# One-core two-layer decoder: layer 0's row maxima and their causal mask in one VectorE instruction with a wide mask

## The chip, the cores and the metric

The kernel runs on one core of one Trainium2 chip. A core has TensorE (PE, with the queue of its weight loads shown as PEld), VectorE (DVE), ScalarE (ACT), GpSimd (POOL) and SyncE (SP), each with its own queue of instructions. Matrix products are written to PSUM; the other operands lie in SBUF. The metric is the device time of one execution in microseconds (us).

## The reference

The program is a decoder trunk of two layers over 1024 positions of width 1024, all in fp32. Layer 0 mixes by multi-head latent attention with 12 heads (query and key 96 wide: 64 without position, 32 with rotary position; values 64 wide), layer 1 by sliding-window attention with sinks and a linear distance bias. Both run memory cross-attention beside it, an output projection and a squared-ReLU MLP. The change lies in layer 0's causal attention:

```python
def one_block(args):
    q_blk, n = args                                   # 128 queries of every head
    t_idx = n * Q_BLOCK + jnp.arange(Q_BLOCK)
    sc = jnp.einsum('bqhd,bkhd->bhqk', q_blk, k) * scale
    mask = k_idx[None, :] <= t_idx[:, None]
    sc = jnp.where(mask[None, None], sc, NEG)         # NEG = -1e30
    p = jax.nn.softmax(sc, axis=-1).astype(v.dtype)
    return jnp.einsum('bhqk,bkhd->bqhd', p, v)
```

The softmax subtracts the maximum of each query's row over the keys that it may see.

## The kernel before, in words

An fp32 matrix is split into a high and a low part (names ending in h and l; ACT makes the high part at L99, DVE the low part at L100), and a product of two such matrices is three products on PE. Layer 0's attention works on scores that are transposed, keys on the partitions and queries along the row, so that the exponentials can go straight into the product with the values. [...] So the maxima are made beforehand from a second, cheaper set of scores that is not transposed.

One "row" of a head is a block of 128 queries: `row_max(h, i)` is row i of head h. It multiplies the high parts of block i's queries with the keys up to and including that block's (`psx`, n = (i+1) x 128 columns, in products of at most 512 columns, L907). A bf16 product of an identity `identb` with a matrix `dmask`, which is 0 on and below the diagonal and -1e30 above it, adds the causal mask to the last 128 columns in PSUM (L908). DVE takes the maximum over the n columns and writes its negative to column i of the head's tile `m8` (`m` in the profile, L909). When a head's eight rows are there, `max_row(h)` transposes m8 on PE (`psxt`, L889), splits it, and two DMAs put it into partition 96 of the head's query tiles `qh`, `ql`. The keys have a row of ones there, so that each transposed score comes out with its maximum taken off.

The main loop goes over (head, block of 128 keys, half of the queries), 12 steps a head. A step has three score products (`pss`, L1030); on diagonal blocks DVE adds the transposed mask `dmaskT` in PSUM (L1038); ACT takes the exponential `p` (L1040); some blocks are split again into `ph`, `pl` (L99, L100). Some steps later the value products go into `pso` (L1060). The values' last 64 columns are ones, so that the row sums come out beside them. The table `WHEN` (L1144) says at which step which row of the next heads' maxima is made: from head 3 on in the order 7, 6, ... 0, psxt last, one row in about one step of the twelve. Rows 4 to 7 of those heads use one PSUM tile with one buffer, rows 0 to 3 share six smaller buffers with the scores. Head 0 has no loop to lie in: its eight rows stand among the last query projections (`psqn`, L109 to L111, copied out at L939) and use a PSUM tile with two buffers.

The outputs of heads are divided by their sums in groups (heads 0 to 5, 6 to 9, 10, 11). DVE takes the reciprocals `rc` (L1119), POOL's queue writes them to DRAM and reads them back spread over 64 partitions each (`rb`, two DMAs for a pair of heads and a half, L1112), and DVE multiplies with them (L1129). `rb` has four buffers.

Within an engine, the order of the instructions is set by a scheduler from the program's order, the dependences and its costs. So taking instructions away can also move others.

Of the kernel before, what the change touches and what calls it, by code (L numbers as in the profile page):

```python
# [9 lines left out]
F32 = mybir.dt.float32  # L10
F32R = mybir.dt.float32r
BF16 = mybir.dt.bfloat16
I32 = mybir.dt.int32
AF = mybir.ActivationFunctionType
ALU = mybir.AluOpType
AX = mybir.AxisListType.X
# [3 lines left out]
P = 128  # L20
D = 1024
S = 1024
# [5 lines left out]
NEG = -1e30  # L28
# [27 lines left out]
def trunk(  # L56
# [7 lines left out]
    nc = tc.nc  # L64
    x = x[0]
    out = out[0]
    mem = mem[0]

    def pool(name, side="left", space=None, bufs=1):
        kw = {"reuse_waits": "tile"}  # L70
        if space is not None:
            kw["space"] = space
        return tc.alloc_tile_pool(name=name, bufs=bufs, side=side, **kw)

    const = pool("const")
# [3 lines left out]
    def ps2(name):  # L79
        return psum[0].tile([P, 1024], F32, tag="s", bufs=2, name=name)  # L80

    def ps1(name):
        return psum[0].tile([P, 512], F32, tag="m", bufs=4 if len(psum) == 1 else 6, name=name)

    def psx(name):
        return ps2(name) if len(psum) == 1 else psum[0].tile([P, 1024], F32, tag="x", bufs=1, name=name)
# [9 lines left out]
    def split(src, hi, lo, scale=None):  # L96

        if scale is None:
            a = nc.scalar.activation(hi, src, AF.Copy)  # L99
            d = nc.vector.tensor_tensor(lo, src, f32(hi), ALU.subtract)  # L100
        else:
            a = nc.scalar.activation(hi, src, AF.Copy, scale=scale)
            d = nc.vector.scalar_tensor_tensor(lo, src, scale, f32(hi), ALU.mult, ALU.subtract)
        return a.ins, d.ins
# [19 lines left out]
    ident = const.tile([P, P], F32, name="ident")  # L124
    nc.gpsimd.memset(ident, 1.0)
    nc.gpsimd.affine_select(out=ident, in_=ident, compare_op=ALU.is_equal, fill=0.0, base=0, pattern=[[-1, P]], channel_multiplier=1)
    identb, dmask = [const.tile([P, P], BF16, name=n) for n in ("identb", "dmask")]
    dmaskT = const.tile([P, P], F32, name="dmaskT")

    def masks(pl):  # L130

        nc.vector.tensor_copy(identb, ident)
        for dst, sgn in ((dmask, 1), (dmaskT, -1)):
            m = pl.tile([P, P], F32, tag="mask", bufs=2, name=f"mask{sgn}")
            nc.gpsimd.memset(m, 0.0)
            nc.gpsimd.affine_select(out=m, in_=m, compare_op=ALU.is_ge, fill=NEG, base=0, pattern=[[-sgn, P]], channel_multiplier=sgn)
            nc.vector.tensor_copy(dst, m)

    eps_t = const.tile([P, 1], F32, name="eps_t")
    nc.gpsimd.memset(eps_t, EPS)  # L140
# [428 lines left out]
    pm = pool("pm", "right")  # L569
# [109 lines left out]
    with tc.issue_after(k_done):  # L679
        put_rope()  # L680
    mp[1].keys(kvt)
    masks(pm)

    for h in range(H):
        nc.gpsimd.memset(padl[(h % 2) * 64 : (h % 2) * 64 + 64, 1 + h // 2 : 2 + h // 2], 0.125 / SLOPES[h])
# [172 lines left out]
    def head_bufs(pl, i):  # L858
        bufs_.append([pl.tile([97, S], F32R, name=f"{n}{i}") for n in ("qh", "ql", "kh", "kl")])

    def head_ones(i):
        if i == 0:
            nc.gpsimd.memset(f32(bufs_[0][2][96:97]), 1.0)
            nc.gpsimd.memset(f32(bufs_[0][3][96:97]), 0.0)
        else:
            for e in (2, 3):
                nc.sync.dma_start(out=f32(bufs_[i][e][96:97]), in_=f32(bufs_[0][e][96:97]))


    def head_tiles(h):  # L870
        r = slice((h % 2) * 64, (h % 2) * 64 + 64)
        q32 = hb.tile([96, S], F32, tag="q32", bufs=1, name=f"q32_{h}")
        k32 = hb.tile([96, S], F32, tag="k32", bufs=1, name=f"k32_{h}")
        nc.sync.dma_start(out=q32[0:64], in_=qn[h // 2][r, :])
        nc.sync.dma_start(out=q32[64:96], in_=qr[h // 4][(h % 4) * 32 : (h % 4) * 32 + 32, :])
        nc.sync.dma_start(out=k32[0:64], in_=kn[h // 2][r, :])
        nc.sync.dma_start(out=k32[64:96], in_=krs)
        qh, ql, kh, kl = bufs_[h % 3]
        if h in (1, 2):
            head_ones(h)  # L880
        split(q32, qh[0:96], ql[0:96])
        split(k32, kh[0:96], kl[0:96])

    m8s = {}

    def max_row(h):
        qh, ql, kh, kl = bufs_[h % 3]
# [11 lines left out]
    def row_max(h, i):  # L899
        if h not in m8s:  # L900
            m8s[h] = hb.tile([P, NT], F32, tag="m8", bufs=2, name=f"m8_{h}")
        qh, ql, kh, kl = bufs_[h % 3]
        n = (i + 1) * P
        ps = psx(f"psx{h}_{i}") if i > 3 or len(psum) == 1 else ps1(f"psx{h}_{i}")
        for a in range(0, n, 512):
            b = min(a + 512, n)
            nc.tensor.matmul(ps[:, a:b], qh[0:96, i * P : (i + 1) * P], kh[0:96, a:b], start=True, stop=b < n, skip_group_check=True)  # L907
        nc.tensor.matmul(ps[:, n - P : n], identb, dmask, start=False, stop=True, skip_group_check=True)  # L908
        nc.vector.reduce_max(m8s[h][:, i : i + 1], ps[:, :n], axis=AX, negate=True)  # L909

    f0 = quad_tile("f0", "qn0")
    qn = [(f0, f1)[j // 4][:, j % 4, :] for j in range(6)]
# [8 lines left out]
    for j in range(6):  # L921
# [4 lines left out]
        ps = ps2(f"pskn{j}")  # L926
# [45 lines left out]
    for n in range(2, 12):  # L972
        q_nope(n // 2, n % 2)
        for i in range(2 * n - 4, min(2 * n - 2, NT)):
            row_max(0, i)
        if n == 7:
            max_row(0)
# [8 lines left out]
    for i in (1, 2):  # L986
        head_bufs(hb1, i)
    at = pool("at", "right")
    vbufs = []
    for i in range(2):  # L990
        vb = (at.tile([P, 4, 128], F32R, name=f"vh{i}"), at.tile([P, 4, 64], F32R, name=f"vl{i}"))
# [5 lines left out]
    def v_tiles(h):  # L997

        vh, vl = vbufs[h % 2]
        src = v[:, 0:4, h * 64 : (h + 1) * 64]  # L1000
        if h < 2:
            nc.gpsimd.memset(f32(vh[:, :, 64:128]), 1.0)
        nc.scalar.activation(vh[:, :, 0:64], src, AF.Copy)
        nc.vector.tensor_tensor(vl, src, f32(vh[:, :, 0:64]), ALU.subtract)
# [102 lines left out]

    def rc_pair(c, j, i):

        rb = at.tile([P, 512], F32, tag="rb", bufs=4, name=f"rb{c}_{j}_{i}")  # L1110
        for e in range(min(2, GRP[c + 1] - GRP[c] - 2 * j)):
            (nc.sync if c == 2 else nc.gpsimd).dma_start(out=rb[e * 64 : e * 64 + 64, :], in_=rc_d[c][2 * j + e, halves[i]].partition_broadcast(64))  # L1112
        return rb
# [18 lines left out]
    def v_full(h):  # L1132
        nc.vector.tensor_copy(vfs[h % 2][:, :, 0:64], v[:, :, h * 64 : (h + 1) * 64])

    wq = WoHalf(0, 0, quad_slots())
    v_tiles(0)
    v_full(0)
    head_tiles(1)

    LV, LB = 3, 5  # L1140
# [13 lines left out]
    for n in range(len(seq) + LB):  # L1154
# [3 lines left out]
        for lag, late in ((LB, True), (LV, False)):  # L1158
            if 0 <= n - lag < len(seq):
                a, b = values(*seq[n - lag], late)  # L1160
# [11 lines left out]
        for g, i in ahead.get(n, ()):  # L1172
            if i < NT:
                row_max(g, i)
            else:
                max_row(g)
        h, j = divmod(n, NB)
# [789 lines left out]
    def feat_mm(w, i, nm, between=None):  # L1967
        ps = ps1(f"psf{nm}_{i}")
        terms = [(w[0][:, k, :], w[1][:, k, :], *xn0.at(k, halves[i])) for k in range(KT)]
        if between is None:  # L1970
            mm3(ps, terms)
        else:
            mm3(ps, terms[:4], last=False)
            between()
            mm3(ps, terms[4:], first=False)
        return ps
# [194 lines left out]
    for n, (c0, sink, j) in enumerate(jobs):  # L2171
# [17 lines left out]
        for i in range(2):  # L2189
            ps = feat_mm(w, i, str(n + 2), None if n < 6 else lambda: next(swa))  # L2190
# [76 lines left out]
```

## Time and profile before

| quantity | value |
|---|---|
| time, median of 3 runs | 2105.88 us (2105.57 to 2107.6) |
| profiled execution, its own time | 2106.59 us |
| its span | 2104.7 us |
| granted TensorE clock, mean | 0.999 |
| matrix products and weight loads | 9842 each |

The span runs from the first to the last instruction of the profiled execution; its own time holds what lies around it too. Layer 0's attention loop starts at about 234 us and ends at about 460 us; head 0's rows stand at 217 to 226 us. A row of a timeline has start, length, engine, line, operation, output and inputs, shapes, and in brackets the idle time before it and who ended it. "x2" means that two such instructions of one kind follow each other. Products on PE overlap, so from one start to the next is less than a product's length.

### The profile page before, as it was taken

Reading aid. Unit: us, or ns where it says so; the run is one execution under the profiler, and the core shown is the slowest. Engines: PE = TensorE matmul, PEld = TensorE weight load, DVE = VectorE, ACT = ScalarE, POOL = GpSimd, SP = SyncE. Lnnn points to the kernel's source line nnn. Section 1 sums busy time; section 2 is a strip of 40 time slices with the busy share of each in tenths; the row PEclk is TensorE's granted clock in tenths of the full one; section 3 lists DMA queues with packets and bytes.
Section 4 is the critical chain, followed back from the end, with each engine's and each line's share of the span. In section 5 each row is a group of like instructions: output and inputs, shape, how many; then the busy total and the mean of one; then the engine's idle time right before and its main releaser. Section 6 shows DMA issues by size and latency. Waiting matters only on the chain.

```text
span 2104.7 us, 28997 instructions
## 1 busy us (share of the span) xinstructions
PE 2084.4 (99%) x9842; PEld 1690.5 (80%) x9842; DVE 1473.9 (70%) x2906; ACT 1112.7 (53%) x2405; POOL 147.4 (7%) x263
## 2 busy tenths in 40 slices
PE   9999999999999999999999999999999999999998
PEld 7888766678888888888888878778788888888887
DVE  8766677775977777976557634666977776976565
ACT  6654466656755444444445434776755444444453
POOL 1001001010000000000001133431000000000000
PEclk9999999999999999999999999999999999999999
DMA  6302223342355446945433634542355446944442
GB/s 218 98 1 76 61 67 92 92 136 100 103 178 165 149 138 231 327 152 156 138 117 104 156 91 123 140 139 81 108 172 165 152 140 235 327 148 155 118 118 90
DMA packets 181796, 292.35 MB, mean 139 GB/s; under 512 B 17691, under 2 KB 71824, under 8 KB 181648
## 3 DMA queue, kind: packets, MB, share of 16 engines
q1 hardware_dynamic: 175152, 272.07, 41.4%
q0 software_dynamic: 5168, 15.80, 2.2%
q10 hardware_dynamic: 1328, 2.63, 0.3%
q8 instruction: 77, 1.26, 0.3%
q14 instruction: 71, 0.58, 0.1%
HBM read 187.34 MB, written 81.18 MB: 128 GB/s over the span
## 4 chain that ended last, share of the span: by engine, by line
PE 90%; DVE 5%; ACT 2%; DMA 1%; issue 1%; POOL 0%; SPq 0%; DVEq 0%; ACTq 0%; POOLq 0%
PE psy L1843 6%; PE psy L1844 6%; PE psy L1842 6%; PE psu L1534 5%; PE psu L1536 5%; PE psu L1535 5%; PE psz L1843 4%; PE psz L1844 4%; PE psz L1842 4%; PE psv L1536 4%; PE psv L1534 4%; PE psv L1535 4%; PE pso L1060 4%; PE pss L1030 3%; PE pswo L111 3%; PE pswo L109 3%
## 5 line engine op out<-in xcount | busy, mean ns | idle before, releaser
L1040 ACT ACTIVATE p<-pss 128x512 f32<-128x512 f32 (+2 forms) x144 | 68.6, 486 | 69.6 <-DVE pss L1038 52.7
L99 ACT ACTIVATE g<-i 128x512 fp32r<-128x512 f32 x79 | 49.8, 631 | 102.8 <-PE psz L1843 45.7
L1842 PE MATMUL psy<-g 128*128 128x512 f32 x256 | 99.9, 390 | 0.0
L1844 PE MATMUL psy<-g 128*128 128x512 f32 x256 | 99.7, 390 | 0.0
L1843 PE MATMUL psy<-g 128*128 128x512 f32 x256 | 99.6, 389 | 0.0
L100 DVE TENSOR_TENSOR g<-i,g 128x512 fp32r<-128x512 f32 x79 | 55.7, 705 | 50.7 <-ACT g L99 50.7
L99 ACT ACTIVATE i<-mr 128x512 fp32r<-128x512 f32 x78 | 47.8, 629 | 72.7 <-PE psu L1535 20.9
L1060 PE MATMUL pso<-p,vf 128*128 128x512 f32 (+2 forms) x192 | 85.4, 527 | 0.5 <-ACT p L1040 0.5
L909 DVE TENSOR_REDUCE m<-psx 128x1 f32<-128x1024 f32 (+7 forms) x96 | 71.9, 751 | 20.0 <-PE psx L908 19.6
L99 ACT ACTIVATE uh<-i 128x512 fp32r<-128x512 f32 x66 | 41.6, 631 | 82.0 <-PE psz L1843 38.3
L100 DVE TENSOR_TENSOR uh<-i,uh 128x512 fp32r<-128x512 f32 x66 | 45.5, 690 | 46.2 <-ACT uh L99 46.1
L1842 PE MATMUL psz<-g 128*128 128x512 f32 x192 | 74.7, 389 | 0.0
L1843 PE MATMUL psz<-g 128*128 128x512 f32 x192 | 74.7, 389 | 0.0
L1844 PE MATMUL psz<-g 128*128 128x512 f32 x192 | 74.7, 389 | 0.0
L1433 ACT ACTIVATE mr<-mr,gcol 128x256 f32<-128x256 f32 (+1 forms) x160 | 63.9, 476 | 13.9 <-DMA mr<-in_mlp_w_up_dram 13.9
L100 DVE TENSOR_TENSOR i<-mr,i 128x512 fp32r<-128x512 f32 x78 | 53.5, 686 | 23.7 <-ACT i L99 23.7
L1030 PE MATMUL pss<-qh,kh 97*128 97x512 f32 (+2 forms) x144 | 67.8, 473 | 0.0
L1030 PE MATMUL pss<-ql,kh 97*128 97x512 f32 (+2 forms) x144 | 58.2, 404 | 0.0
L1754 DVE TENSOR_TENSOR mqq<-mqf,mqq 128x512 f32<-128x512 f32 x64 | 43.0, 685 | 20.1 <-DMA mqf<-in_mlp_w_down_dram 20.0
L1842 PEld LDWEIGHTS psy<-g 128*128 128x128 f32 x256 | 48.1, 188 | 9.9
L1843 PEld LDWEIGHTS psy<-g 128*128 128x128 f32 x256 | 48.1, 188 | 9.9
L1844 PEld LDWEIGHTS psy<-g 128*128 128x128 f32 x256 | 48.1, 188 | 9.9
(648 smaller groups left out, 6858.3 us busy)
## 6 DMA issues: line engine op xcount, KB each, us to landing
i<-hd SPq DMA_DIRECT2D x154, 256.0 KB
hd<-uh SPq DMA_DIRECT2D x76, 256.0 KB
hd<-ul SPq DMA_DIRECT2D x76, 256.0 KB
mr<-in_mlp_w_up_dram SPq DMA_DIRECT2D x36, 512.0 KB
hd<-x SPq DMA_DIRECT2D x72, 256.0 KB
mr<-hd SPq DMA_DIRECT2D x70, 256.0 KB
d<-in_mlp_w_up_dram SPq DMA_DIRECT2D x32, 512.0 KB
mqf<-in_mlp_w_down_dram SPq DMA_DIRECT2D x32, 512.0 KB
```

Source lines behind the costliest of these rows:

```text
L99: a = nc.scalar.activation(hi, src, AF.Copy)
L100: d = nc.vector.tensor_tensor(lo, src, f32(hi), ALU.subtract)
L909: nc.vector.reduce_max(m8s[h][:, i : i + 1], ps[:, :n], axis=AX, negate=True)
L1030: return lambda: nc.tensor.matmul(o, a, b, skip_group_check=True, **kw)
L1040: nc.scalar.activation(p[:, c0:], ps, AF.Exp, scale=SC)
L1060: mms.append(lambda: nc.tensor.matmul(o, a, b, skip_group_check=True, **kw))
L1534: nc.tensor.matmul(ps, wh[:, k, :], xh[:, k, :], start=p in (1, 2, 5) and k == 0, stop=False, skip_group_check=True)
L1535: nc.tensor.matmul(ps, wh[:, k, :], xl[:, k, :], start=False, stop=False, skip_group_check=True)
L1536: nc.tensor.matmul(ps, wl[:, k, :], xh[:, k, :], start=False, stop=k == 3, skip_group_check=True)
L1842: nc.tensor.matmul(ps, ah[:, j, :], bh, start=p in (1, 5, 2) and k == 0, stop=False, skip_group_check=True)
L1843: nc.tensor.matmul(ps, ah[:, j, :], bl, start=False, stop=False, skip_group_check=True)
L1844: nc.tensor.matmul(ps, al[:, j, :], bh, start=False, stop=k == NP - 1, skip_group_check=True)
```

## The change

The mask product is gone, and with it `identb` and the bf16 mask. `dmask` and `dmaskT` are fp32 and POOL writes them directly. A tile `wide` of 128 x 1024 holds zeros in its first 896 columns and the mask in its last 128; its last n columns are the mask of a row that is n wide. For heads from 1 on, one DVE instruction (`tensor_tensor_reduce`) adds the mask to the whole row, changes the sign by its factor -1, writes the row back to where it was in PSUM, and takes the minimum into m. For head 0, whose rows come before the pool that holds `wide` is open, a plain reduction takes the columns ahead of the last block, and the fused instruction takes the last block with the narrow `dmask`, starting from the plain reduction's result. To make room, `rb` has two buffers in place of four. In the order and the profile the fused instruction has two parts: the operation itself, and a read of its accumulator into m.

```diff
-    identb, dmask = [const.tile([P, P], BF16, name=n) for n in ("identb", "dmask")]
-    dmaskT = const.tile([P, P], F32, name="dmaskT")
-
-    def masks(pl):
-
-        nc.vector.tensor_copy(identb, ident)
-        for dst, sgn in ((dmask, 1), (dmaskT, -1)):
-            m = pl.tile([P, P], F32, tag="mask", bufs=2, name=f"mask{sgn}")
-            nc.gpsimd.memset(m, 0.0)
-            nc.gpsimd.affine_select(out=m, in_=m, compare_op=ALU.is_ge, fill=NEG, base=0, pattern=[[-sgn, P]], channel_multiplier=sgn)
-            nc.vector.tensor_copy(dst, m)
+    dmask, dmaskT = [const.tile([P, P], F32, name=n) for n in ("dmask", "dmaskT")]
+
+    def mask(dst, sgn):
+
+        nc.gpsimd.memset(dst, 0.0)
+        d = dst[:, dst.shape[1] - P :]
+        nc.gpsimd.affine_select(out=d, in_=d, compare_op=ALU.is_ge, fill=NEG, base=0, pattern=[[-sgn, P]], channel_multiplier=sgn)
...
-    masks(pm)
+    mask(dmask, 1)
+    mask(dmaskT, -1)
...
-            nc.tensor.matmul(ps[:, a:b], qh[0:96, i * P : (i + 1) * P], kh[0:96, a:b], start=True, stop=b < n, skip_group_check=True)
-        nc.tensor.matmul(ps[:, n - P : n], identb, dmask, start=False, stop=True, skip_group_check=True)
-        nc.vector.reduce_max(m8s[h][:, i : i + 1], ps[:, :n], axis=AX, negate=True)
+            nc.tensor.matmul(ps[:, a:b], qh[0:96, i * P : (i + 1) * P], kh[0:96, a:b], start=True, stop=True, skip_group_check=True)
+        m = m8s[h][:, i : i + 1]
+        least = 3.0e38
+        if h == 0 and i:
+            nc.vector.reduce_max(m, ps[:, : n - P], axis=AX, negate=True)
+            least = m
+        o, k = (ps[:, n - P : n], dmask) if h == 0 else (ps[:, :n], wide[0][:, S - n :])
+        nc.vector.tensor_tensor_reduce(o, o, k, -1.0, least, ALU.add, ALU.min, accum_out=m)
...
+    wide.append(at.tile([P, S], F32, name="wide"))
...
-        rb = at.tile([P, 512], F32, tag="rb", bufs=4, name=f"rb{c}_{j}_{i}")
+        rb = at.tile([P, 512], F32, tag="rb", bufs=2, name=f"rb{c}_{j}_{i}")
...
+    mask(wide[0], 1)
     head_tiles(1)
```

The order of the instructions moves in few places; behind about 445 us nothing does. On PE in a steady head the mask's weight load and product fall out from between row 7 of head 6 (`psx6_7`) and the scores that stand behind it. Before:

```order
L907 MATMUL psx6_7_3450<-kh0_1966,qh0_1964 128x512 x2
L908 LDWEIGHTS identb_66
L908 MATMUL psx6_7_3450<-dmask_67,identb_66 128x128
L1030 MATMUL pss4_1_7_3455<-qh1_2531,kh1_2533 128x128
L1060 MATMUL pso4_0_3388<-pl4_0_1_3379,vh0_2542 128x384
L1030 MATMUL pss4_1_7_3455<-ql1_2532,kh1_2533 128x128
L1060 MATMUL pso4_0_3388<-ph4_0_2_3408,vh0_2542 128x256
```

After:

```order
L904 MATMUL psx6_7_3408<-kh0_1960,qh0_1958 128x512 x2
L1033 MATMUL pss4_1_7_3412<-qh1_2524,kh1_2526 128x128
L1063 MATMUL pso4_0_3348<-pl4_0_1_3340,vh0_2536 128x384
L1033 MATMUL pss4_1_7_3412<-ql1_2525,kh1_2526 128x128
L1063 MATMUL pso4_0_3348<-ph4_0_2_3367,vh0_2536 128x256
L1033 MATMUL pss4_1_7_3412<-qh1_2524,kl1_2527 128x128
```

The neighbours are otherwise the same, and row 6 (`psx6_6`) still comes nine products further on. On DVE at the same place, before:

```order
L1038 TENSOR_TENSOR pss4_0_3_3437<-pss4_0_3_3437,dmaskT_68 128x128
L909 TENSOR_REDUCE m8_6_3449<-psx6_7_3450 128x1
L100 TENSOR_TENSOR pl4_0_3_3446<-p4_0_3_3443,ph4_0_3_3445 128x128
L1038 TENSOR_TENSOR pss4_1_7_3455<-pss4_1_7_3455,dmaskT_68 128x128
L909 TENSOR_REDUCE m8_6_3449<-psx6_6_3472 128x1
L909 TENSOR_REDUCE m8_6_3449<-psx6_5_3494 128x1
```

After:

```order
L1041 TENSOR_TENSOR pss4_0_3_3395<-pss4_0_3_3395,dmaskT_67 128x128
L911 ISA psx6_7_3408,m8_6_3407<-psx6_7_3408,wide_2535 128x1024
L911 ISA m8_6_3407 128x1
L100 TENSOR_TENSOR pl4_0_3_3404<-p4_0_3_3401,ph4_0_3_3403 128x128
L1041 TENSOR_TENSOR pss4_1_7_3412<-pss4_1_7_3412,dmaskT_67 128x128
L911 ISA psx6_6_3429,m8_6_3407<-psx6_6_3429,wide_2535 128x896
L911 ISA m8_6_3407 128x1
L911 ISA psx6_5_3450,m8_6_3407<-psx6_5_3450,wide_2535 128x768
L911 ISA m8_6_3407 128x1
```

Each plain reduction became the fused instruction over the whole row with the read of its accumulator right behind it. On PE at the end of head 0's rows, between its last row (`psx0_7`) and the transpose of the maxima (`psxt0`), before:

```order
L110 MATMUL psqn3_0_2447<-cTl_560,wqn2h_2104 128x512
L111 MATMUL psqn3_0_2447<-cTh_559,wqn2l_2105 128x512
L109 MATMUL psqn3_1_2458<-cTh_559,wqnh_2102 128x512
L110 MATMUL psqn3_1_2458<-cTl_560,wqnh_2102 128x512
L111 MATMUL psqn3_1_2458<-cTh_559,wqnl_2103 128x512
L109 MATMUL psqn3_1_2458<-cTh_559,wqnh_2102 128x512
L110 MATMUL psqn3_1_2458<-cTl_560,wqnh_2102 128x512
L111 MATMUL psqn3_1_2458<-cTh_559,wqnl_2103 128x512
L109 MATMUL psqn3_1_2458<-cTh_559,wqn2h_2104 128x512
L110 MATMUL psqn3_1_2458<-cTl_560,wqn2h_2104 128x512
L111 MATMUL psqn3_1_2458<-cTh_559,wqn2l_2105 128x512
L889 MATMUL psxt0_2469<-ident_63,m8_0_2377 8x128
```

After:

```order
L904 MATMUL psx0_6_2430<-kh0_1960,qh0_1958 128x512
L904 MATMUL psx0_6_2430<-kh0_1960,qh0_1958 128x384
L904 MATMUL psx0_7_2435<-kh0_1960,qh0_1958 128x512 x2
L111 MATMUL psqn3_1_2451<-cTh_553,wqnl_2097 128x512
L109 MATMUL psqn3_1_2451<-cTh_553,wqn2h_2098 128x512
L110 MATMUL psqn3_1_2451<-cTl_554,wqn2h_2098 128x512
L111 MATMUL psqn3_1_2451<-cTh_553,wqn2l_2099 128x512
L886 MATMUL psxt0_2462<-ident_63,m8_0_2371 8x128
L109 MATMUL psqn4_0_2469<-cTh_553,wqnh_2096 128x512
```

Before, fourteen projection products stand between the last row's mask and the transpose (the last eleven are shown); after, four. On DVE the last rows of head 0, before:

```order
L909 TENSOR_REDUCE m8_0_2377<-psx0_4_2416 128x1
L909 TENSOR_REDUCE m8_0_2377<-psx0_5_2421 128x1
L939 COPY qn0_1956<-psqn2_1_2426 128x512
L909 TENSOR_REDUCE m8_0_2377<-psx0_6_2437 128x1
L909 TENSOR_REDUCE m8_0_2377<-psx0_7_2442 128x1
L939 COPY qn0_1956<-psqn3_1_2458 128x512
L100 TENSOR_TENSOR mhl0_2471<-psxt0_2469,mhl0_2471 8x128
```

After:

```order
L911 ISA m8_0_2371 128x1
L911 ISA psx0_5_2414,m8_0_2371<-psx0_5_2414,dmask_66,m8_0_2371 128x128
L911 ISA m8_0_2371 128x1
L908 TENSOR_REDUCE m8_0_2371<-psx0_6_2430 128x1
L908 TENSOR_REDUCE m8_0_2371<-psx0_7_2435 128x1
L911 ISA psx0_6_2430,m8_0_2371<-psx0_6_2430,dmask_66,m8_0_2371 128x128
L911 ISA m8_0_2371 128x1
L911 ISA psx0_7_2435,m8_0_2371<-psx0_7_2435,dmask_66,m8_0_2371 128x128
L911 ISA m8_0_2371 128x1
L941 COPY qn0_1950<-psqn3_1_2451 128x512
L100 TENSOR_TENSOR mhl0_2464<-psxt0_2462,mhl0_2464 8x128
```

The two last plain reductions stand next to each other, the fused instructions of their last blocks behind both.

More of the change, by code (lines that the diff above doesn't have):

```diff
@@ L882, in head_tiles @@
         split(k32, kh[0:96], kl[0:96])
-    m8s = {}
+    m8s, wide = {}, []
     def max_row(h):
```

## The prediction

> **What bounds the kernel now.** I read first the page's span, busy shares and chain, then the costliest groups, then windows of single heads, then the timeline around one row of maxima.
>
> ```profile
> span 2104.7 us, 28997 instructions
> PE 2084.4 (99%) x9842; PEld 1690.5 (80%) x9842; DVE 1473.9 (70%) x2906; ACT 1112.7 (53%) x2405; POOL 147.4 (7%) x263
> PE 90%; DVE 5%; ACT 2%; DMA 1%; issue 1%; POOL 0%; SPq 0%; DVEq 0%; ACTq 0%; POOLq 0%
> ```
>
> PE is busy for 99% of the span and carries 90% of the chain, so an instruction taken from PE is worth its time wherever PE is really the limit. VectorE (DVE) has 30% free, but as an average only. The next question is which engine is the limit in the stretches where rows of maxima are made: a steady head (rows of head 6), and heads 0 and 1 of the score loop (rows of heads 1 and 2).
>
> ```profile
> 301.36:318.85 17.49, 17.49 (x88) 12.22 (x87) 12.41 (x26) 10.97 (x22) 0.00 (x0) 1.00 0.27 62
> ...
> 234.40:251.90 17.50, 16.24 (x82) 11.36 (x81) 16.29 (x31) 11.09 (x22) 1.78 (x4) 1.00 0.36 84
> 251.90:266.30 14.40, 14.40 (x70) 9.52 (x69) 12.01 (x24) 9.39 (x19) 0.00 (x0) 1.00 0.38 84
> ```
>
> The columns are the stretch, its length, then busy time of PE, PE's weight loads, DVE, ACT and POOL, the granted clock (1.00), and DMA. In the steady head PE has no gap (17.49 of 17.49) and DVE 12.41. In head 0 DVE has 16.29 of 17.50 and PE idles 1.26: there DVE is the limit. In head 1 it is PE again.
>
> **The mask product in a steady head (A).** What does one of them hold PE for?
>
> ```profile
> 307.50 1.02 PE L1060 MATMUL pso<-p,vf 128*128 128x512 f32 x2
> 307.96 0.80 PE L1030 MATMUL pss<-ql,kh 97*128 97x512 f32 x1
> ...
> 308.84 0.46 PE L907 MATMUL psx<-kh,qh 96*128 96x512 f32 x2
> 309.13 0.23 PE L908 MATMUL psx<-dmask,identb 128*128 128x128 bf16 x1
> 309.17 0.48 PE L1030 MATMUL pss<-qh,kh 97*128 97x512 f32 x1
> 309.49 0.40 PE L1030 MATMUL pss<-ql,kh 97*128 97x512 f32 x1
> 309.72 0.39 PE L1030 MATMUL pss<-qh,kl 97*128 97x512 f32 x1
> ...
> 310.19 0.23 PE L908 MATMUL psx<-dmask,identb 128*128 128x128 bf16 x1
> 310.26 1.08 PE L1060 MATMUL pso<-p,vf 128*128 128x512 f32 x2
> 310.77 0.74 PE L1030 MATMUL pss<-qh,kh 97*128 97x384 f32 x1
> ```
>
> Products overlap, so I go from start to start. The mask's own slot is 0.04 (309.13 to 309.17) and 0.07 (310.19 to 310.26). But the product behind it is also longer: 309.17 to 309.49 is 0.32 where the same shape next takes 0.23, and the pair p by vf takes 0.51 (310.26 to 310.77) against 0.46 (307.50 to 307.96). Together 0.13 and 0.12; I take 0.12. Eight rows a head give 8 x 0.12 = 0.96 us.
>
> That holds if PE stays the limit. One place in each head is not PE's own: rows 4 to 7 share one PSUM tile, so row 6's products wait until row 7 has been reduced.
>
> ```profile
> 300.00 0.69 PE L907 MATMUL psx<-kh,qh 96*128 96x512 f32 x2
> 300.53 0.23 PE L908 MATMUL psx<-dmask,identb 128*128 128x128 bf16 x1
> 300.80 1.23 DVE L909 TENSOR_REDUCE m<-psx 128x1 f32<-128x1024 f32 x1 [0.30 <-PE psx L908]
> 302.08 0.30 PEld L907 LDWEIGHTS psx<-kh,qh 96*128 96x128 f32 x2 [0.30 <-DVE m L909]
> ```
>
> Before, 2.08 us from product to product: DVE starts 0.80 after, works 1.23, and PE goes on 0.05 behind. The new instruction isn't in this trace at 1024 columns, but layer 1 runs the same operation (an add with a running minimum, shown as CUSTOM_DVE_ANT_0, and a read of its accumulator).
>
> ```profile
> L909 DVE TENSOR_REDUCE m<-psx 128x1 f32<-128x1024 f32 x12 | 14.6, 1217 | 1.9 <-PE psx L908 1.8
> L909 DVE TENSOR_REDUCE m<-psx 128x1 f32<-128x256 f32 x12 | 5.0, 416 | 0.0
> L2094 DVE CUSTOM_DVE_ANT_0 sp<-psw,df,sinks_b 128x256 f32<-128x256 f32 x84 | 36.2, 479 | 17.1 <-PE psw L2090 15.4 <-POOL sp L2114 1.6
> L2094 DVE CUSTOM_DVE_ANT_0 sp<-psw,df,sinks_b 128x128 f32<-128x128 f32 x12 | 3.6, 347 | 1.7 <-PE psw L2090 1.7
> L1038 DVE TENSOR_TENSOR pss<-pss,dmaskT 128x128 f32<-128x128 f32 x96 | 27.9, 293 | 20.3 <-PE pss L1030 19.5 <-ACT ph L99 0.6
> ...
> 1303.31 0.48 DVE L2094 CUSTOM_DVE_ANT_0 sp<-psw,df,sinks_b 128x256 f32<-128x256 f32 x1
> 1303.71 0.08 DVE L2094 DVE_READ_ACCUMULATOR2_ANT sst<- 128x1 f32 x1
> 1303.71 0.48 DVE L2094 CUSTOM_DVE_ANT_0 sp<-psw,df,sinks_b 128x256 f32<-128x256 f32 x1
> ```
>
> 128 columns more cost 479 - 347 = 132 ns, that is 1.03 ns a column; for 1024 columns 347 + 7 x 132 = 1271 ns, against 1217 for the plain reduction. The read of 0.08 starts together with the next instruction, 0.40 after the fused one began, so it lies inside its last 0.08 and costs almost nothing. Row 7 to row 6 after the change: DVE starts about 0.73 after (0.07 of mask gone), 1.27, then 0.01 for the read's end and 0.05: 2.06 instead of 2.08. PE alone would now be 2.08 - 0.12 = 1.96 there, so 0.10 of the 0.96 is given back and 0.86 stays. Rows of heads 3 to 11 make nine such heads: 9 x 0.86 = -7.7 us. Bounds: 0.06 a mask (the slot alone, with the 0.10) -3.4; 0.13 -8.5.
>
> [...]
>
> **Head 0's rows (B)** are made among the query projections, and there the change adds work to DVE: two instructions a row.
>
> ```profile
> 217.49 0.67 DVE L909 TENSOR_REDUCE m<-psx 128x1 f32<-128x128 f32 x2 [0.32 <-PE psx L908]
> 218.96 3.02 DVE L909 TENSOR_REDUCE m<-psx 128x1 f32<-128x384 f32 x4 [0.80 <-PE psx L908]
> 221.91 0.68 DVE L939 COPY qn<-psqn 128x512 f32<-128x512 f32 x1
> 222.50 2.21 DVE L909 TENSOR_REDUCE m<-psx 128x1 f32<-128x896 f32 x2
> ...
> 226.12 0.27 PE L889 MATMUL psxt<-ident,m 128*8 128x128 f32 x1
> ```
>
> Each plain reduction is one block shorter, so the widths 128 to 1024 become 128 to 896: the one of 1.217 falls away. Eight fused ones of 0.347 come, 2.78. DVE's chain grows by 1.56, and by some 0.06 for each of seven waits for its own m (an estimate from the 0.05 that PE took behind DVE above). It ended at 224.71, while the transpose of the maxima (psxt) stood in PE's order for 226.12: 1.41 of cover. Now it ends at about 226.6. On PE eight masks go (1.0), so PE would be at psxt at 225.1 and waits about 1.5. What stands behind psxt is the same 36 products in both orders, so the stage ends about 0.5 later. I take +0.5. Bounds: -1.0 where DVE still hides it (its idle 0.80 at 218.96 refilled), +1.5 where the two instructions of a row don't overlap at all.
>
> **Rows of heads 1 and 2 (C).** In head 0 of the loop DVE is the limit. A fused row of 256 columns lets its successor start after 0.40; a plain one, by the rows above, after 0.416 less the same 0.08 of overlap, 0.33. That is +0.07 a row, +0.56 for the eight rows of that stretch. In the next stretch PE is the limit and the 12.01 of DVE leaves room: of 0.96 for the masks I take off 4 x 0.06 for the rows 4 to 7 on the shared tile, -0.7. The two make 0 within their error. Bounds: -1.5, where the idle 1.26 of PE takes up DVE's part and the masks pay in both, to +1.3, where nothing of the second comes and DVE's starts don't overlap (8 x 0.08 more).
>
> **The buffers rb from 4 to 2 (D).** The third pair of reciprocals now waits on POOL until the first product with rb is over, and the other two queue behind it.
>
> ```profile
> 424.00 4.11 POOL L1112 DMA_DIRECT2D rb<-rcd  x8 [1.43 <-DMA rcd<-rc]
> rb<-rcd POOLq DMA_DIRECT2D x8, 128.0 KB, 3.0
> ...
> 427.58 0.69 DVE L1129 TENSOR_TENSOR qn<-rb,qn 128x512 f32<-128x512 f32 x1 [2.64 <-DMA rb<-rcd]
> 429.54 0.69 DVE L1129 TENSOR_TENSOR fa<-rb,fa 128x512 f32<-128x512 f32 x1 [0.20 <-DMA rb<-rcd]
> 431.15 0.30 DVE L1038 TENSOR_TENSOR pss<-pss,dmaskT 128x128 f32<-128x128 f32 x1 [0.24 <-PE pss L1030]
> ...
> 434.85 0.81 PE L1060 MATMUL pso<-p,vf 128*128 128x384 f32 x2
> ```
>
> The first product ends at 428.27; two issues of 0.51 and 3.0 to land put the third at about 432, not 429.54, and the add of 431.15 behind it at about 432.6. It is 1.45 late and ends at 432.9; its block's value product, behind one exponential, stands on PE for 434.85, so 1.95 are left for that one exponential. I count 0; bound +1.45 if that cover is gone. In the earlier group (353 us) nothing stands right behind the products: 0.
>
> **Edits at nothing (E).** Three DVE copies of setup go, where PE is the limit; the most they can bring is their own time. POOL fills the wide mask behind the fills of vf and vh.
>
> ```profile
> 234.73 1.00 POOL L995 MEMSET vf<- 128x512 f32 x2 [26.23 <-PE psqn L111]
> ```
>
> 1024 columns take 1.00 there, POOL is 7% busy, and the first fused row of head 1 comes behind two adds, an exponential and PE's products of the first blocks; I count 0, bound +1.0, one such fill.
>
> **Sum.** -7.7 + 0.5 + 0 + 0 + 0 = -7.2. The profiled execution took 2106.59 us (span 2104.7), so 2099.4; it lies 0.71 above the median of 2105.88, and by that median it is 2098.7 us.
>
> **The rivals.**
>
> R1, slower: the fused instruction writes its whole row back into PSUM, and layer 1's writes into SBUF. Should that cost more than 1.03 ns a column, row 7 would hold the shared tile for longer. At twice the price row 7 takes 347 - 132 = 215 ns and 1024 x 2.06, 2.32 us, 1.05 more in nine heads (+9.5); the 4608 columns of a head are +4.7 in head 0 of the loop and about +2.3 beyond DVE's room in head 1; head 0's own eight blocks +1.05. That is +17.5 on -7.2: +10.3, 2116.2 us. It decides from 7.2/17.5 of the extra 1.03, about 0.42 ns more a column. Against it: the add of L1038 writes in place into PSUM and takes 293 for 128 columns, less than the fused 347.
>
> R2, no change that can be told: PE gets only the mask's own slot back (0.055), because what I booked on the next product belongs to any change of shape. 9 x (0.44 - 0.10) = -3.1, with B -2.6: 2103.3 us. Against it: the same 0.09 and 0.05 behind masks of different neighbours.
>
> R3, less gain: the fused instruction, its read and the successor run one after the other. Then each row costs 0.083 more on DVE: 9 rows 7 (0.75), sixteen rows of heads 1 and 2 (1.3), eight of head 0 (0.65), 2.7 in all: -4.5, 2101.4 us. The trace speaks against it, by the read and the next instruction that both start at 1303.71. By that it would be weighed low; but there the successors don't depend on each other, and here PE waits for the read. [...]
>
> **How the numbers follow.** Measurements of this kernel tell about 0.2% (4.2 us) from nothing. Forecast 0.67, all of it faster; R3 0.13, two thirds of it faster; R2 0.11, same; R1 0.09, slower. So faster 0.76, same 0.15, slower 0.09. The range: below, masks at 0.13 (-8.5) with the low ends of B and C (-1.0, -1.5) are -11: 2095.0; above it holds R3 and R2 and ends a little past them, at 2104.5. Outside are R1 and the corners.
>
> **What would show it.** Right: a steady head of about 16.6 us with PE still full; fused 1024 at about 1.27 us and its read at 0.08; PE waiting some 0.1 for the fused row 7 before row 6; psxt of head 0 near 226.6 behind a wait of about 1.5; head 0 of the loop at 17.5 give or take 1. R1 would show as fused 1024 of 1.7 us or more, R2 as a head above 17.1 with PE full, R3 as reads that stand behind the fused instruction rather than inside it. Wrong in another way: a wait for rb on the chain at 430 us, or PE starved by a fused row other than row 7.

## The result, and the profile after

The changed kernel takes 2101.21 us in the median of 16 runs (2099.6 to 2104.0), the kernel before 2106.02 us in 16 (2104.88 to 2107.85): -4.8 us, a ratio of 0.9977 (0.997 to 0.9984). Forecast were 2098.7 and the range 2095.0 to 2104.5. So the direction and the range were right, and a third of the gain is missing. The profiled execution took 2103.57 us, with a span of 2100.7, 4.0 below that of before; it is one of the slower runs, and the reason for that is part of what follows.

The page of the changed kernel:

```profile
span 2100.7 us, 28955 instructions
PE 2076.4 (99%) x9746; PEld 1691.2 (81%) x9746; DVE 1475.8 (70%) x3006; ACT 1111.9 (53%) x2405; POOL 148.5 (7%) x265
PE 89%; DVE 6%; ACT 2%; DMA 2%; issue 1%; SPq 0%; POOL 0%; DVEq 0%; ACTq 0%
```

PE is busy for 8.0 us less, but the span fell by 4.0 only: the other half became gaps on PE. The windows of a steady head (rows of head 6), from one transpose of maxima to the next, and of the start of the loop, from the first scores to `psxt1` and from there to `psxt2`:

```profile
295.96:312.63 16.67, 16.67 (x79) 12.29 (x77) 12.56 (x33) 10.86 (x23) 0.00 (x0) 1.00 0.28 64
...
234.31:250.81 16.50, 14.52 (x67) 10.43 (x66) 15.94 (x37) 10.87 (x21) 2.19 (x5) 1.00 0.38 89
250.81:263.97 13.16, 13.16 (x58) 9.17 (x57) 11.45 (x30) 8.51 (x18) 0.00 (x0) 1.00 0.42 92
```

The start of the loop before, cut at the same places (the prediction's windows there are cut elsewhere):

```profile
234.41:250.54 16.13, 14.87 (x74) 10.23 (x73) 15.58 (x29) 10.46 (x21) 1.78 (x4) 1.00 0.39 91
250.54:264.64 14.10, 14.10 (x65) 9.27 (x65) 11.50 (x22) 8.97 (x18) 0.00 (x0) 1.00 0.39 84
```

A steady head went from 17.49 to 16.67 us, and PE still has no gap in it. The group of the widest fused rows, and the place where the next row waits for row 7, on DVE and on PE:

```profile
L911 DVE CUSTOM_DVE_ANT_0 psx<-psx,wide 128x1024 f32<-128x1024 f32 x11 | 13.5, 1227 | 1.7 <-PE psx L904 1.7
```

```profile
298.30 1.23 DVE L911 CUSTOM_DVE_ANT_0 psx<-psx,wide 128x1024 f32<-128x1024 f32 x1 [0.21 <-PE psx L904]
299.45 0.14 DVE L911 DVE_READ_ACCUMULATOR2_ANT m<- 128x1 f32 x1
299.45 0.28 DVE L100 TENSOR_TENSOR pl<-p,ph 128x128 fp32r<-128x128 f32 x1
```

```profile
297.58 0.68 PE L904 MATMUL psx<-kh,qh 96*128 96x512 f32 x2
...
299.64 0.68 PE L904 MATMUL psx<-kh,qh 96*128 96x512 f32 x2
```

The fused instruction over 1024 columns takes 1227 ns where the plain reduction took 1217, though it also writes the row back to PSUM. The read of the accumulator takes 0.14, but starts together with the next instruction, and from row 7 to row 6 it is 2.06 us (297.58 to 299.64). What PE waits for, from 205 to 460 us:

```profile
PE psx L904 <- DVE m L911: 2.1, 3, 1.1
PE psxt L886 <- DVE m L911: 1.4, 1, 1.4
PE pso L1063 <- ACT ph L99: 0.7, 1, 0.7
PE pso L1063 <- ACT p L1043: 0.7, 1, 0.7
```

The 1.4 is head 0's transpose (at 226.01), as forecast. The single wait of 1.1 for a row is new, in the head after the first group of reciprocals:

```profile
365.29 0.69 DVE L1132 TENSOR_TENSOR qn<-rb,qn 128x512 f32<-128x512 f32 x1 [1.20 <-DMA rb<-rcd]
365.90 0.29 DVE L1041 TENSOR_TENSOR pss<-pss,dmaskT 128x128 f32<-128x128 f32 x1
366.10 1.23 DVE L911 CUSTOM_DVE_ANT_0 psx<-psx,wide 128x1024 f32<-128x1024 f32 x1
```

```profile
364.30 0.68 PE L904 MATMUL psx<-kh,qh 96*128 96x512 f32 x2
...
367.44 0.67 PE L904 MATMUL psx<-kh,qh 96*128 96x512 f32 x2 [1.05 <-DVE m L911]
```

A product with rb waits 1.20 for its transfer, DVE's queue stands, and behind it stand an add and the row 7 that PE needs. The largest loss comes after the loop. Windows of the tail, first of before, then of the changed kernel (the column ahead of the last two is the granted clock):

```profile
444.00:446.00 2.00, 1.29 (x6) 0.66 (x5) 1.91 (x5) 1.64 (x7) 0.00 (x0) 1.00 0.89 320
446.00:448.00 2.00, 1.84 (x7) 0.80 (x6) 1.91 (x5) 1.28 (x4) 0.00 (x0) 1.00 1.05 400
448.00:450.00 2.00, 2.00 (x10) 1.66 (x10) 1.91 (x5) 0.78 (x2) 0.00 (x0) 1.00 0.64 231
```

```profile
438.00:440.00 2.00, 1.14 (x6) 0.62 (x5) 1.91 (x5) 1.90 (x8) 0.00 (x0) 1.00 0.93 325
440.00:442.00 2.00, 2.00 (x6) 1.14 (x7) 1.94 (x4) 1.01 (x3) 0.00 (x0) 0.85 1.04 390
442.00:444.00 2.00, 2.00 (x7) 1.54 (x6) 1.94 (x6) 1.05 (x3) 0.00 (x0) 0.50 0.47 172
444.00:446.00 2.00, 2.00 (x9) 1.60 (x8) 1.97 (x6) 2.00 (x3) 0.00 (x0) 0.80 0.00 0
```

PE's gaps here are a little larger after the change, and then the granted clock is 0.50 for about 3.4 us, in which PE does 7 products in 2 us in place of 10. Further on, where the second half of the output projection begins, PE waits once more; before, its product at 489.83 had no wait ahead of it:

```profile
485.68 0.50 PE L109 MATMUL pswo<-g,d 128*128 128x512 f32 x1 [0.78 <-DVE i L1411]
```

Measured as PE's lead over before, in this profile: 7.28 us at the last scores, 6.69 at 438.89 (0.6 lost in gaps), 5.15 at 444.78 (1.5 lost by the clock), 4.02 at 486.48 (1.1 lost about this wait).

With starts read from the timelines, every profile can be cut at the same instructions. All numbers are us; "tail" goes from the first product of the last diagonal scores of head 11 (at 441.31 before) to one and the same output product further on (at 524.74 before), and the 19.7 us between psxt11 and the tail are the same in all; "gaps" is the sum of PE's idle times over 0.08 in its first 25 us. The kernels other than before and after are those of the next section.

| kernel | first projection to first scores | loop, to psxt2 | psxt2 to psxt8 | psxt8 to psxt9 | psxt9 to psxt11 | tail | gaps | clock falls |
|---|---|---|---|---|---|---|---|---|
| before | 28.78 | 30.23 | 103.68 | 17.59 | 35.72 | 83.43 | 0.87 | no |
| before, again | 28.78 | 30.25 | 103.69 | 17.64 | 35.69 | 83.44 | 0.86 | no |
| after | 29.43 | 29.66 | 98.71 | 17.76 | 33.92 | 86.71 | 1.10 | yes |
| products kept | 28.81 | 30.63 | 104.11 | 17.56 | 35.71 | 87.89 | 2.91 | yes |
| head 0 as before | 28.81 | 29.67 | 98.77 | 17.39 | 33.96 | 86.19 | 1.37 | yes |
| before, 2 rb | 28.81 | 29.81 | 103.67 | 17.48 | 35.55 | 87.59 | 2.66 | yes |
| after, rb steps 4 | 29.43 | 29.62 | 98.94 | 17.93 | 34.07 | 85.03 | 1.08 | no |
| small tiles, 2 rb | 29.40 | 29.62 | 98.76 | 17.29 | 34.23 | 84.51 | 0.74 | no |
| 3 rb | 29.40 | 29.77 | 98.72 | 17.60 | 34.25 | 85.65 | 1.37 | yes |
| 4 rb | 29.40 | 29.66 | 98.75 | 17.03 | 34.35 | 83.73 | 0.95 | no |
| 4 rb, again | 29.40 | 29.62 | 98.69 | 17.04 | 34.01 | 84.91 | 1.09 | yes |
| 4 rb, later psxt0 | 27.94 | 29.66 | 98.82 | 16.85 | 34.09 | 83.42 | 0.88 | no |
| the same, again | 27.92 | 29.64 | 98.72 | 16.87 | 34.18 | 85.00 | 1.07 | yes |
| after, filled | 29.40 | 29.66 | 98.69 | 17.43 | 34.10 | 84.89 | 0.75 | no |

What lies behind the tail is alike in all of them (within 0.8 us). What lies ahead varies by 2.4 us from profile to profile (the first projection starts between 203.45 and 205.89), with no pattern by kernel.

### The profile page after: what moved, and what is told of

Same layout as the page of the kernel before. It is cut to its first block, busy times and chain, and to the rows that moved or that the text cites. A ratio compares the mean times of both kernels' runs of the same rounds, so it can differ in the third digit from the quotient of the medians.

```text
span 2100.7 us, 28955 instructions
## 1 busy us (share of the span) xinstructions
PE 2076.4 (99%) x9746; PEld 1691.2 (81%) x9746; DVE 1475.8 (70%) x3006; ACT 1111.9 (53%) x2405; POOL 148.5 (7%) x265
## 4 chain that ended last, share of the span: by engine, by line
PE 89%; DVE 6%; ACT 2%; DMA 2%; issue 1%; SPq 0%; POOL 0%; DVEq 0%; ACTq 0%
PE psy L1848 6%; PE psy L1847 5%; PE psy L1846 5%; PE psu L1538 5%; PE psu L1540 5%; PE psu L1539 5%; PE psz L1847 4%; PE psz L1846 4%; PE psz L1848 4%; PE psv L1539 4%; PE psv L1538 4%; PE psv L1540 4%; PE pso L1063 3%; PE pss L1033 3%; PE pswo L109 2%; PE pswo L111 2%
## 5 line engine op out<-in xcount | busy, mean ns | idle before, releaser
L911 DVE CUSTOM_DVE_ANT_0 psx<-psx,wide 128x1024 f32<-128x1024 f32 (+6 forms) x88 | 66.6, 760 | 16.2 <-PE psx L904 16.2
```

The costliest lines, as they stand in the source:

```text
L911: nc.vector.tensor_tensor_reduce(o, o, k, -1.0, least, ALU.add, ALU.min, accum_out=m)
```

## Experiments

**What do the products cost, and what the rest?** Two kernels with the same DVE work, that differ by 88 mask products. Head 0 is as before in both; the first masks heads 1 to 11 twice.

```diff
+        if True:                                  # keepmask;  h0old: if h == 0
+            nc.tensor.matmul(ps[:, n - P : n], identb, dmask, start=False, stop=True, skip_group_check=True)
+        if h == 0:
+            nc.vector.reduce_max(m8s[h][:, i : i + 1], ps[:, :n], axis=AX, negate=True)
+            return
```

> The changed kernel with the mask products put back for all heads (head 0 as it was before, with mask product and plain reduction; heads 1 to 11 masked twice, by PE and by the fused instruction). It prices everything but the missing products. Theory (a mask product holds PE for 0.12 us): a steady head goes back from 16.67 to about 17.5, nine heads +7.5, heads 1 and 2 +1.0 against the same kernel without the products (next run): about 2109. Rival (a mask product costs only its own slot of 0.055 us): +4, about 2104.5, steady head about 17.1.

> The changed kernel with head 0's eight rows as before (mask product and one plain reduction). Theory (head 0's two-step rows made their stage about 0.66 us longer, PE waits 1.4 us for the last maximum): about 2100.5, and no wait of PE for the maxima before head 0's transpose. Rival (the stage lost nothing, the 0.66 is the start of the run): 2101.2.

Measured: 2110.73 us (11 runs) with the products, 2100.56 (7 runs) without; ratios to before 1.002 (1.0011 to 1.0029) and 0.9974 (0.9963 to 0.9984). Windows of a steady head, with and without:

```profile
298.10:315.66 17.56, 17.56 (x87) 12.22 (x85) 12.63 (x33) 10.97 (x23) 0.00 (x0) 1.00 0.27 61
```

```profile
296.42:313.10 16.68, 16.68 (x79) 12.30 (x77) 12.57 (x33) 10.86 (x23) 0.00 (x0) 1.00 0.28 64
```

Eight products make 0.88 us, 0.11 each: the rival with the own slot of 0.055 alone falls. The difference of the two medians is 10.2 us for 88 products; the stages of the two profiles differ by 9.9, 1.7 of it in the tail. Against before (17.49) the fused rows with products kept are 0.07 slower per head: the fused instruction by itself is a small loss, all the gain is PE's. Head 0 as before brings 0.62 in its stage (29.43 to 28.81), as expected, and 0.65 in the median, which its scatter doesn't resolve.

**The two buffers alone.** The kernel before with one number changed:

```diff
-        rb = at.tile([P, 512], F32, tag="rb", bufs=4, name=f"rb{c}_{j}_{i}")
+        rb = at.tile([P, 512], F32, tag="rb", bufs=2, name=f"rb{c}_{j}_{i}")
```

> The kernel before with two buffers for rb in place of four, nothing else. Theory (in the group after head 6 a late rb holds DVE, and behind it the row 7 that PE waits for, about 1.05 us): 2107.1, with PE waiting about 1 us for a row 7 near 373 us. Rival (rb is covered as the prediction had it, the wait seen in the changed kernel is chance): 2106.0.

Measured: 2108.94 us (11 runs), ratio 1.0014 (1.0005 to 1.0023). It costs 2.7, more than expected, and in another place. There is no late row 7 (17.48 for that head, as before); the whole loss is in the tail, 87.59 in place of 83.43. DVE there:

```profile
430.16 0.69 DVE L1129 TENSOR_TENSOR fa<-rb,fa 128x512 f32<-128x512 f32 x1 [1.48 <-DMA rb<-rcd]
...
434.53 0.94 DVE L1119 RECIPROCAL rc<-den 8x128 f32<-8x128 f32 x1 [2.09 <-DMA den<-on]
...
439.88 0.68 DVE L1129 TENSOR_TENSOR fa<-rb,fa 64x512 f32<-64x512 f32 x1 [0.76 <-DMA rb<-rcd]
```

The waits of PE there, and the windows with the clock:

```profile
PE pso L1060 <- DVE pl L100: 0.8, 1, 0.8
PE pswo L111 <- DVE x L100: 0.7, 1, 0.7
PE pswo L109 <- ACT x L99: 0.7, 1, 0.7
PE pso L1060 <- ACT ph L99: 0.5, 1, 0.5
```

```profile
444.00:446.00 2.00, 1.47 (x7) 1.07 (x6) 1.91 (x5) 1.96 (x7) 0.00 (x0) 0.74 0.89 324
446.00:448.00 2.00, 1.65 (x5) 0.83 (x3) 1.94 (x4) 0.78 (x2) 0.00 (x0) 0.50 1.05 400
448.00:450.00 2.00, 1.68 (x4) 1.39 (x5) 2.00 (x7) 2.00 (x3) 0.00 (x0) 0.50 0.44 156
450.00:452.00 2.00, 2.00 (x6) 1.57 (x6) 1.94 (x5) 1.15 (x3) 0.00 (x0) 0.56 0.01 4
```

The third product with rb comes 2.85 us later against PE's place than before (430.16 + 2.23 for the lead of this run is 432.39, before it was 429.54). It makes the adds late, these the exponentials, these head 10's copy on ACT, and that the transfer of its sums: its reciprocals start at 434.53 where PE's lead would have them at 432.75. Their products with rb then wait again (0.76) and stand ahead of `pl`, for which PE waits. PE's gaps sum to 2.66 in place of 0.87, and the clock is at half for some 6.8 us: of the 4.16 that the tail is longer, 1.8 are gaps and the rest goes with the clock.

In the changed kernel the same transfer is as late (425.17, with its lead of 7.28, is 432.45), but the delay ends there. Its ACT makes head 10's copy (`on`) ahead of the exponential that waits for the late add; in the kernel before with two buffers it stands behind it. First the changed kernel, then the kernel before with two buffers:

```profile
424.66 0.59 ACT L1089 ACTIVATE on<-pso 65x512 f32<-65x512 f32 x1 [0.40 <-PE pso L1063]
426.10 0.77 ACT L1043 ACTIVATE p<-pss 128x384 f32<-128x384 f32 x2 [0.85 <-DVE pss L1041]
```

```profile
431.09 0.49 ACT L1040 ACTIVATE p<-pss 128x384 f32<-128x384 f32 x1 [1.79 <-DVE pss L1038]
431.48 0.58 ACT L1086 ACTIVATE on<-pso 65x512 f32<-65x512 f32 x1
```

So head 10's reciprocals aren't late in the changed kernel: they start at 427.69, which is 434.97 with its lead, and before it was 434.98.

```profile
427.69 0.94 DVE L1122 RECIPROCAL rc<-den 8x128 f32<-8x128 f32 x1 [0.29 <-DMA den<-on]
```

**Fewer products with rb per step**, so that two buffers might do (the first group has room for it):

```diff
-        if n % 2 or n > 11 * NB:
+        if n % 4 == 1 or n > 11 * NB:
```

> The changed kernel with the products with rb at every fourth step of the loop in place of every second, so that two buffers suffice. Theory: the wait of 1.05 us for a late row 7 near 367 us goes: 2100.2. Rival: nothing there costs time, 2101.2. In all four profiles I look at 430 to 450 us as well: theory 'chance', the drop of the granted clock after the loop (0.72 over 6 us in the changed kernel's profile, about 1.9 us lost) shows in some of the profiles only; theory 'system', it shows in each kernel with fused rows.

Measured: 2101.69 us (11 runs), 0.9977 (0.9968 to 0.9986), no gain. The wait for row 7 stayed (17.93 for that head, PE waits 1.2 there). But the edit hardly reached the order: by the two profiles the orders on PE, ACT and POOL are those of the changed kernel, and on DVE two other instructions move, so that one product with rb stands one place later. So this run says nothing about wider spacing; it is in effect the changed kernel once more, with 0.48 between the medians. Of the first four profiles of this section the clock fell in three, the kernel before with two buffers among them, and not in this one. So the fall doesn't belong to the fused rows, and it doesn't come in every run of one order either.

**Four buffers again.** To make room, wide is bf16 (zeros and -1e30 need no more for this purpose), the split maxima have one buffer, and dmask lies in a pool that is released; the first kernel is the control with all this and two buffers.

```diff
-    wide.append(at.tile([P, S], F32, name="wide"))
+    wide.append(at.tile([P, S], BF16, name="wide"))
...
-        rb = at.tile([P, 512], F32, tag="rb", bufs=2, name=f"rb{c}_{j}_{i}")
+        rb = at.tile([P, 512], F32, tag="rb", bufs=4, name=f"rb{c}_{j}_{i}")
```

> The changed kernel with smaller side tiles (wide in bf16, one buffer for the split maxima, dmask in a pool that is released) and still two buffers for rb: the control for the next run. Both theories: 2101.2 within 0.7, and from the last head's scores to a fixed product behind the loop about 86 us, as in the changed kernel (86.7) and not as before (83.4).

> The same with four buffers for rb, as before the change. Theory (the two buffers cost the tail behind the loop about 3.3 us and a late row 7 in the head after the first group 1.0): tail 83.4, that head 16.7, 2097.0. Rival (the tail is long because PE reaches it earlier than the transfers, whatever the buffers): tail stays at about 86, 2100.5 at the best.

> The changed kernel with wide in bf16 and three buffers for rb. Theory: the four transfers of the second group need one wait for a buffer instead of two, so the tail loses less than with two: 2098 to 2100. Rival: as with two, 2101.2.

Measured: two buffers 2101.07 us (10 runs, as the changed kernel), three 2099.97 (11 runs), four 2099.57 (6 runs, ratio 0.997, 0.9959 to 0.9982). Four buffers bring 1.5, not the 4 expected. The control's tail was 84.51 and not 86: in its profile the clock did not fall. It has the wait of 0.8 at the second half of the output projection, as the changed kernel has, and the kernels with three and four buffers don't have it: that alone is 1.1 of what they gain. The head with the late row 7 shrank from 17.29 in the control (17.76 in the changed kernel) to 17.03, where 16.7 was expected; PE still waits 0.31 there. The tail with four was 83.73. Three lie within the 2098 to 2100 that were expected, though in their profile the clock fell (tail 85.65) and that head is 17.60.

**The best version: head 0's transpose later.** On top of four buffers, one number:

```diff
-        if n == 7:
+        if n == 8:
             max_row(0)
```

> As the run with four buffers, and head 0's transpose of the maxima one projection (nine products) later in the program. Theory (PE waits 1.4 us there for the last fused row, since the two-step rows lengthen DVE's chain): the wait goes, 1.4 us less than with four buffers alone, about 2095.6. Rival (the maxima then come too late for the first scores at 234 us, by their DMA): PE waits there instead, no gain.

Measured: 2099.43 us, no difference to four buffers alone (2099.57), but from 5 runs that spread from 2095.91 to 2100.43; its profile, on the other hand, had the stage at 27.94 as expected. Both were measured a second time, side by side:

> Four buffers for rb a second time, for the comparison with the next run on the same chip: 2099.6.

> Four buffers and the later transpose of head 0's maxima a second time. Theory (the stage from the first projection to the first scores is 1.46 us shorter in the profile, 27.94 against 29.40): 1.0 to 1.5 below the run beside it, about 2098.3. Rival (the gain is given back before the end, as in the medians of the first time): the same as the run beside it.

Measured: 2099.37 us and 2097.59 us (5 runs each), 0.9968 (0.9956 to 0.9981) and 0.9959 (0.9947 to 0.9972) of before. All runs of each together have medians of 2099.5 (11 runs) and 2098.2 (10 runs). The stage is 1.48 shorter in the second profile, too, so the gain in the stage is shown; in the whole time it was 0.1 the first time and 1.8 the second, and the intervals overlap. PE's wait of 1.3 for head 0's last maximum is there with four buffers alone; with the later transpose the largest waits are others:

```profile
PE psxt L885 <- DVE m L910: 1.3, 1, 1.3
```

```profile
PE psx L903 <- DVE m L910: 1.4, 2, 0.7
PE pso L1064 <- ACT p L1044: 0.9, 1, 0.9
PE pso L1064 <- ACT ph L99: 0.6, 1, 0.6
```

In these second profiles the clock fell in both, with four buffers and gaps of 1.09 and 1.07, and the tails were 84.91 and 85.00 in place of 83.73 and 83.42. So four buffers don't exclude the fall.

**More work on PE in the gaps.** The changed kernel with six needless products at the start of the output projection (the group's first real product overwrites them):

```diff
+                if layer == 0 and half == 0 and p < 2:
+                    for _ in range(3):
+                        nc.tensor.matmul(ps, terms[0][0], terms[0][2], start=True, stop=True)
```

> The changed kernel with six more products on PE (1.4 us of work, their results overwritten) at the start of the output projection behind the loop, where PE had gaps of 0.23, 0.70 and 0.17 us in the changed kernel's profile. Theory (the granted clock falls to 0.5 for about 3.4 us when PE's gaps there sum to about 1.1 us or more, which costs 1.7): the gaps shrink to some 0.5, no row of a granted clock under 1 near 441 us, the tail from the last head's scores is about 85.5 us in place of 86.7, time 2100.5: more work, less time. Rival (the clock's fall has another cause, such as the kernel's position in time): it stays, and the time is 2101.2 to 2102.5.

Measured: 2100.52 us (10 runs, 2099.15 to 2103.81), 0.9974 (0.9965 to 0.9984). Windows of its tail:

```profile
436.00:438.00 2.00, 1.35 (x8) 0.84 (x6) 1.88 (x5) 1.51 (x7) 0.00 (x0) 1.00 0.97 291
438.00:440.00 2.00, 1.90 (x10) 1.28 (x9) 1.93 (x4) 1.19 (x3) 0.00 (x0) 1.00 1.06 398
440.00:442.00 2.00, 2.00 (x9) 1.65 (x10) 1.91 (x6) 0.87 (x2) 0.00 (x0) 1.00 0.72 271
```

Its gaps are 0.75, the clock stays at 1.00, and its tail is 84.89 with 1.4 us more work, against 86.71. In the time it is 0.7 less than the changed kernel, which the spread of both doesn't settle; that more work wasn't slower here is what it shows.

**The kernel before, a second profile.**

> The kernel before, unchanged, for a second profile. Theory (the tail behind the loop depends on PE's gaps, and before the change they sum to 0.87 us and the clock holds): gaps of 0.8 to 1.0 us, no fall of the granted clock at 448 us, tail 83.4 us. Rival (the fall comes by chance in any kernel): it may show here as well, with a tail of about 85.

Measured: 2105.11 us in one run, no fall, gaps 0.86, tail 83.44 against 83.43. The two profiles of the kernel before agree here to 0.01. That doesn't mean that its clock never falls: the mean granted clock of every run is on record, it is 0.998 in the seven profiles in which the clock falls behind the loop and 0.999 in the seven in which it doesn't, and 14 of the 65 other runs of the kernel before show 0.998 too, with medians that are 1.1 to 2.2 us longer. Where in these runs it fell isn't on record, and 0.999 doesn't exclude a short fall, since 0.001 of 2100 us is 4.2 us at half the clock.

## Why the prediction was right, and where it failed

**What bounds, and A.** Right. PE has no gap in a steady head, before and after; 0.86 a head was forecast, 0.82 measured (17.49 to 16.67), and a product costs 0.11 (0.12 taken). From psxt2 to psxt11, nine heads, the two profiles differ by 6.60 where 7.7 was forecast; the late row 7 in one head, which D left out, makes up for nearly all of the rest (the head from psxt8 to psxt9 grew by 0.17 in place of falling by 0.82).

**Row 7 to row 6.** 2.06 us forecast, 2.06 measured, though two parts were a little off and cancel: 1.23 for the fused row (1.27), and a read of 0.14 (0.08), which ends 0.06 behind the fused row (0.01). R1 (PSUM output at a higher price) falls with the group's 1227 ns, R3 (the fused instruction, its read and the successor one after the other) with the two rows at 299.45: what stands behind the read starts with it, 1.15 after a fused instruction of 1.23 began. R3's time, 2101.4, lies nearest to the measured one, but by chance: what is missing of the gain stands elsewhere. With the products kept, the fused rows alone lose 0.07 a head. R2 falls with the 0.88 for eight products.

**B.** +0.5 forecast, +0.65 measured (28.78 to 29.43), with the wait of 1.4 that was forecast as 1.5.

**C.** 0 forecast within -1.5 to +1.3, -0.57 measured (30.23 to 29.66): +0.37 for head 0 and -0.94 for head 1, by the two signs that the working had.

**D is the step that failed**: "I count 0; bound +1.45 if that cover is gone", and "In the earlier group (353 us) nothing stands right behind the products: 0." In the earlier group an add and row 7 stood behind a late product with rb, and PE waited 1.05 us. The two buffers alone don't do that: with the mask products on PE that head is 17.48 and 17.56 with two buffers, and without them PE still waits 0.31 with four. It takes the two together, in the head that had become shorter on PE. In the second group the cover held in the changed kernel, as said: the third product with rb is 2.9 late, head 10's reciprocals are not. In the kernel before with two buffers it didn't hold, by the order on ACT, and D by itself costs 2.7 us, part of it by the clock. What two buffers cost behind the loop in the changed kernel is the wait at 485.68, 1.1 us, for which the runs show the circumstances and not the mechanism. Taken away from the changed kernel, D gives 1.5 to 1.7. The working followed the late transfer to the product that reads it, and in the earlier group not to what stands behind that product in DVE's queue.

**Where the missing 2.4 us are.** By the two profiles, against the terms of the sum: A 1.1 less than forecast (the late row 7), B 0.15 worse, C 0.57 better, and 1.7 behind the loop without the clock's part (0.6 in gaps, 1.1 about 485.68). That is 2.4, the distance from -7.2 to -4.8. The sum had no term for the granted clock. Its fall costs 1.5 in the changed kernel's profile, and that profile is 2.4 us above the median; but 4 of the 16 runs of the changed kernel have a mean clock of 0.998, and 14 of 65 of the kernel before, so the clock doesn't make the difference of the medians. With four buffers the gain is 6.5 us (2099.5 against 2106.0), near the sum of 7.2.

**What stays open.** The write of head 10's reciprocals to DRAM was followed by its read 1.3 us after the issue in both profiles of before and in some changed kernels, and 2.3 to 2.6 after in others, the changed kernel's own (428.66 to 431.29) among them, with four buffers as with two. It makes the last products with rb later, by up to 0.8 us of waiting (with three buffers), and the 0.6 that the changed kernel loses in gaps behind the loop stands behind such waits; why it takes either time isn't known. The wait of 0.8 at 485.68 shows in the profiles with two buffers and without the mask products in the loop, in none of the others; the buffer that the product takes there is freed by an add on DVE, and why these kernels take that one wasn't followed up. What starts the clock's fall is told only in part by the sums of gaps, as the last section shows.

## What to carry to other kernels

Follow a late buffer past its first consumer: to what stands behind it in the queue of the engine that waits, then through the queue of the next engine, up to the point where nothing covers. Whether the delay gets through hangs on the order there: one copy ahead of an exponential or behind it decided here whether head 10's reciprocals came at their time (434.97 with the lead, 434.98 before) or 1.78 us late (434.53 for 432.75). Room that a change takes from other tiles is a term of its own; here it ate a quarter of the gain (1.5 to 1.7 us of 6.5), and a mask of zeros and -1e30 in bf16, with two smaller savings, gave the room back. And see from the order that an edit moved what it was meant to move, before its time is read.

## What the runs showed of the hardware

In the tail the granted clock of PE fell to 0.50 without any long gap. No single gap there was longer than 1.1 us, in the changed kernel 0.70, yet the clock fell in all five profiles with gaps that sum to 1.10 and more, in none of six with 0.95 and less, and in two of three between 1.07 and 1.09. In the changed kernel it was at half from 441.4 to 444.8, 3.4 us; in the kernel before with two buffers, with gaps of 2.66, for about 6.8 (445.0 to 451.8), twice that.

The gaps alone don't decide. Of three profiles with nearly equal sums the clock held in one (1.08) and fell in two (1.07 and 1.09), and no run shows what made the difference. And in the changed kernel PE waited 1.35 us in one piece ahead of 226.01, longer than any gap of the tail, and the clock stayed at 1.00.

The runs with a mean clock of 0.998 and less fit with the gaps where these are large: 8 of 11 for the kernel before with two buffers and 8 of 11 with the products kept (gaps of 2.66 and 2.91), 4 of 16 for the changed kernel, 1 of 10 with its gaps filled, but 5 of 11 with four buffers, where the two profiles have 0.95 and 1.09.
